# A two-layer block with four token mixers: 512-column products for values and output, fourteen merge-gate pairs ahead of the attention, one score scale on GpSimd

## The chip, the core and the metric

The kernel runs on one core of a Trainium2 chip. TensorE (PE) multiplies, VectorE (DVE), ScalarE (ACT) and GpSimd (POOL) do the elementwise work, SyncE's queue (SP) issues the DMAs. The metric is the device time of one execution in microseconds; a kernel's figure is the median of its runs.

## The reference

Two layers of the following, on 1024 tokens of width 1024, all in float32. `x` goes in, `x + rms_norm(merged @ w_o)` comes out.

```python
h = rms_norm(x, g_pre)
parts = jnp.split(h @ w_in, IN_SPLITS, axis=-1)          # a_u, a_v, ..., c_v, ..., m_z
y_a = chunked_gmlp(a_u, a_v, ...) * silu(a_z)            # local gated MLP on chunks of 128 tokens
y_b = nsa_attention(...) * silu(b_z)                     # compressed + selected + window of 256, three gates
y_c = forgetting_attention(...) * silu(c_z)              # causal, with forget gates
y_m = memory_attention(...) * silu(m_z)                  # 256 memory tokens
up = jnp.einsum('bsnw,nwd->bsnd', ys, w_br)              # four branches, 512 -> 1024 each
gates = sigmoid(jnp.einsum('bsd,dne->bsne', h, w_gate))  # four gates of 1024 x 1024
merged = jnp.einsum('bsnd,bsnd->bsd', gates, up)
return x + rms_norm(merged @ w_o, g_post)
```

## The kernel before, in words

Each float32 operand is split into two parts (`hi`, rounded to the type that TensorE takes, and `lo`, the rest), and a product is three matmuls: hi·hi, hi·lo, lo·hi (`mm3`, L240). A weight comes as a block of 128 x 1024 by DMA into `wr` (2 buffers), ACT makes `wh` (L220), POOL makes `wl` (L222); both have 3 buffers. For the names in `mk` and `mv` (the memory weights) POOL makes only the first half of `wl`, DVE the second (L224). An accumulation takes one PSUM bank of 512 columns: 2 banks `pj` and 3 banks `s`.

A layer runs through these stages, in program order; a scheduler at build time interleaves them and fixes each engine's order:

1. `front`: the memory's keys and values, the pre-norm of the tokens into `hh`, `hl` (two halves of 512 tokens).
2. `gates`: the values of the gated MLP (`gmlp_v`, names `av`) and of the forgetting attention (`put_values`, names `cv`), each in two column halves of 256; per half and for each of 8 token tiles 24 matmuls of 256 columns (`proj_t`, L271). `token_sums` meanwhile makes sums of the tokens on POOL, ACT and POOL, in four steps that stand between these projections. `gmlp_w` loads and splits the MLP's mixing weights (`wsr`, `wsh`, `wsl`, `ab`). Then `FRONT`, a list of gate pairs (n, e): `gate_pair` computes two gate blocks (n, e) and (n, e+1) for all tokens with 7 quarter products of 12 matmuls instead of 8, by sums of tokens and of weights (`weight_sums`), and stores them to DRAM (`thd`). After each pair a further small piece runs (`among`: the forget gates, then eight `gmlp_mix`).
3. `attention`: the compression, the forgetting attention (`fox`), projections, then the three-way attention (`nsa`, 64 units over both layers). In an NSA unit the selected and the window scores are exponentiated on ACT, scaled by 1/sum times a gate on DVE (`scale`, L640), turned by TensorE (L597), split by ACT and DVE, and multiplied with the values (L609). Between the units' matmuls stand those of `FILL`: names of independent projections. `u`, `c`, `m`, `b` finish branches; `w` and `y` are single gate blocks of branch 0 and 2 (`gate_early`), 48 matmuls of 512 columns each. A pace rule ties them evenly to the marks of the attention's score matmuls.
4. `merge`: four `add_branch`, which load the stored gates, or compute a gate that is not yet made, and sum; then `out_proj` for two token halves: four column quarters of `wo`, for each 4 token tiles of 24 matmuls with 256 columns.

Before, `FRONT` has 9 pairs (18 blocks) and `FILL` 13 single blocks; the 32nd, (2, 5), is computed in the merge.

`order_slots` (L167) adds a rule for all tiles of one pool: the first write of a tile waits for the first write of the tile that the program asked for before it in the same place.

## Time and profile before

| | us |
|---|---|
| median of 3 runs (lowest, highest) | 3187.17 (3183.8, 3191.8) |
| the profiled execution | 3185.2 |
| its span in the trace | 3183.4 |
| busy: PE, DVE, ACT, POOL | 3071.0, 1845.6, 1484.6, 1433.3 |

The profiled execution took 1.8 us more than its span and lies 2 us under the median. Matmuls are pipelined: one with 512 columns is shown as some 390 ns long although the next starts much sooner, so PE's busy time is a union of overlapping rows, and what a matmul costs is read from the distance of two starts. L numbers are lines of the kernel before.

### The profile page before, as it was taken

What the parts mean: (1) busy time and instruction counts of PE and PEld (TensorE: products, weight loads), DVE (VectorE), ACT (ScalarE), POOL (GpSimd) and SP (SyncE); (2) the same over time, 40 slices, a digit from 0 to 9 for tenths busy, and PEclk for the clock granted to TensorE, in tenths of its full rate; (3) what the DMA queues carried; (4) which work ended last, traced back from release to release, by engine and by line L of the source; (5) the groups of instructions that cost most, each with busy time, mean ns of one, the idle gap of its engine ahead of it and who ended that gap; (6) DMA issues with size and microseconds to landing.
All of it is one profiled execution on the core that took longest, in us unless ns stands there. A gap on an engine that the chain in (4) does not pass through costs nothing.

```text
span 3183.4 us, 48317 instructions
## 1 busy us (share of the span) xinstructions
PE 3071.0 (96%) x16704; PEld 2633.9 (83%) x16704; DVE 1845.6 (58%) x4329; ACT 1484.6 (47%) x3393; POOL 1433.3 (45%) x1142
## 2 busy tenths in 40 slices
PE   6999999999999999999989999999999999999998
PEld 6978877887888888788989788888888888887888
DVE  6255447768666855336551554477685678554363
ACT  4333335556556555313443433455665556552132
POOL 6744445543232323258557444445432333232673
PEclk9999999999999999999999999999999999999999
DMA  6334485654334322456553344955632342225454
GB/s 206 101 116 133 135 249 172 189 179 131 103 104 147 109 90 93 149 173 197 193 180 105 113 135 146 276 160 175 192 123 83 107 153 99 98 90 184 156 185 140
DMA packets 251685, 466.96 MB, mean 147 GB/s; under 512 B 42512, under 2 KB 100880, under 8 KB 251440
## 3 DMA queue, kind: packets, MB, share of 16 engines
q1 hardware_dynamic: 251440, 463.87, 45.7%
q8 instruction: 132, 2.16, 0.3%
q14 instruction: 113, 0.93, 0.1%
HBM read 326.35 MB, written 137.43 MB: 146 GB/s over the span
## 4 chain that ended last, share of the span: by engine, by line
PE 78%; DVE 5%; POOL 5%; issue 4%; DMA 4%; ACT 3%; SPq 1%; DVEq 0%; POOLq 0%; ACTq 0%
PE pj L244 12%; PE pj L248 12%; PE pj L247 12%; PE s L247 6%; PE s L244 6%; PE s L248 6%; PE s L447 5%; PE o L609 5%; PE pt L597 5%; PE pj L447 4%; PE s L565 3%; PE s L566 3%; POOL wl L222 2%; DVE p L638 1%; POOL acc L1291 1%
## 5 line engine op out<-in xcount | busy, mean ns | idle before, releaser
L222 POOL TENSOR_TENSOR wl<-wr,wh 128x1024 fp32r<-128x1024 f32 (+1 forms) x216 | 515.9, 2392 | 646.5 <-ACT wh L220 562.5
L244 PE MATMUL pj<-hh,wh 128*128 128x512 f32 x1648 | 651.4, 395 | 2.6 <-DVE z L317 1.5
L248 PE MATMUL pj<-hh,wl 128*128 128x512 f32 x1648 | 651.4, 395 | 1.6 <-POOL wl L222 1.6
L247 PE MATMUL pj<-hl,wh 128*128 128x512 f32 x1648 | 649.7, 394 | 0.0
L575 ACT ACTIVATE p<-p,nm 128x384 f32<-128x384 f32 (+3 forms) x512 | 306.8, 601 | 204.3 <-DVE nm L570 201.3
L308 DVE TENSOR_TENSOR pt<-pt,pt 128x512 fp32r<-128x512 f32 (+1 forms) x464 | 292.4, 635 | 147.7 <-ACT pt L306 146.1
L248 PEld LDWEIGHTS pj<-hh,wl 128*128 128x128 f32 x1648 | 310.2, 188 | 61.6 <-POOL wl L222 2.5
L244 PEld LDWEIGHTS pj<-hh,wh 128*128 128x128 f32 x1648 | 310.8, 189 | 60.8 <-DVE z L317 2.4
L247 PEld LDWEIGHTS pj<-hl,wh 128*128 128x128 f32 x1648 | 310.4, 188 | 57.7
L306 ACT ACTIVATE pt<-pt 128x512 fp32r<-128x512 f32 (+1 forms) x464 | 251.9, 554 | 222.8 <-PE pt L597 162.2
L220 ACT ACTIVATE wh<-wr 128x1024 fp32r<-128x1024 f32 x216 | 228.4, 1057 | 248.0 <-PE pj L247 84.8
L609 PE MATMUL o<-pt,v 128*128 128x512 f32 (+1 forms) x864 | 245.2, 370 | 7.6 <-DVE pt L308 7.3
L618 POOL TENSOR_TENSOR yt<-yt 128x256 f32<-128x256 f32 x128 | 100.6, 786 | 292.7 <-ACT yt L617 232.8
L597 PE MATMUL pt<-ident,p 128*128 128x128 f32 x1488 | 230.9, 272 | 0.3
L597 PEld LDWEIGHTS pt<-ident,p 128*128 128x128 f32 x1488 | 184.9, 140 | 42.5 <-DVE pt L308 0.7
L244 PE MATMUL s<-yh,wh 128*128 128x512 f32 x512 | 199.9, 393 | 7.1 <-ACT yh L306 5.3
L247 PE MATMUL s<-yl,wh 128*128 128x512 f32 x512 | 201.0, 393 | 1.5 <-DVE yl L310 1.4
L248 PE MATMUL s<-yh,wl 128*128 128x512 f32 x512 | 200.3, 391 | 0.0
L565 PE MATMUL s<-kd,q 128*128 128x512 f32 (+2 forms) x512 | 187.5, 369 | 13.1 <-DVE nm L570 13.1
L566 PE MATMUL s<-kl,q 128*128 128x512 f32 (+2 forms) x512 | 175.7, 345 | 0.0
L609 PEld LDWEIGHTS o<-pt,v 128*128 128x128 f32 x864 | 147.6, 188 | 32.0 <-DVE pt L308 12.3
L640 DVE TENSOR_SCALAR p<-p,r,sg 128x384 f32<-128x384 f32 (+2 forms) x320 | 167.0, 577 | 1.7
(370 smaller groups left out, 7143.1 us busy)
## 6 DMA issues: line engine op xcount, KB each, us to landing
wr<-wt SPq DMA_DIRECT2D x234, 512.0 KB
th<-thd SPq DMA_DIRECT2D x124, 256.0 KB
thd<-gu SPq DMA_DIRECT2D x72, 256.0 KB
q<-rq SPq DMA_DIRECT2D x32, 512.0 KB
yf<-y SPq DMA_DIRECT2D x64, 256.0 KB
thd<-th SPq DMA_DIRECT2D x52, 256.0 KB
vd<-vs SPq DMA_DIRECT2D x48, 256.0 KB
v<-vd SPq DMA_DIRECT2D x24, 512.0 KB
```

The source lines that it names most:

```text
L222: nc.gpsimd.tensor_sub(lo[:, :n], raw[:, :n], hi.bitcast(F32)[:, :n])
L244: ins = nc.tensor.matmul(out, ah, bh, start=k == 0, stop=False)
L247: nc.tensor.matmul(out, ah, bl, start=False, stop=False)
L248: nc.tensor.matmul(out, al, bh, start=False, stop=k == n - 1)
L306: self.last_act = nc.scalar.activation(hi, src, AF.Copy, scale=scale)
L308: (nc.gpsimd if pool else nc.vector).tensor_sub(lo, src, hi.bitcast(F32))
L447: nc.tensor.matmul(out, w[a][:, k], t[b][:, k], start=start and k == x == 0, stop=k == 3 and x == 2, skip_group_check=True)
L565: self.mark(nc.tensor.matmul(ps[:, :w], q[:, tq], kd[:, b0:b0 + w], start=True, stop=False), 1 + n / 128)
L566: nc.tensor.matmul(ps[:, :w], q[:, tq], kl[:, b0:b0 + w], start=False, stop=True)
L575: nc.scalar.activation(p[:, :n], p[:, :n], AF.Exp, bias=init, scale=-1.0, accum_out=l[:, x:x + 1])
L597: nc.tensor.transpose(pt[:, off + x * 128:off + x * 128 + 128], src, self.ident)
L609: nc.tensor.matmul(o[:, :, t0:t0 + m], it["v"], w[:, :, off:off + m], start=first, stop=last)
```

## The change

- `av`, `cv` and `wo` are laid out in full 512 columns, four blocks of two k-slices each (form "C"), and go through a new `proj_wide`: for four token tiles it holds four PSUM banks at once and goes through the weight's four parts; the bank of a tile is complete with the last part. It is called once per token half (so each `av` and `cv` weight is loaded twice) or, for `wo`, once per column half and token half.
- `wl` of `av` and `cv` is made half by POOL and half by DVE.
- `gmlp_w` stands behind the first `gmlp_v` instead of ahead of it.
- `FRONT` has 14 pairs (all of n = 0, 3, 1 and (2, 0), (2, 2)), `FILL` keeps the four single blocks y4 to y7.
- The window's scale in an NSA unit runs on GpSimd.
- The squares of the output go to a tile of their own instead of the bank's other half.

```diff
@@ gates
-    for h in range(2):
-        wide(f"cv{h}", "in", OFF["c_v"] + h * 256 + r(256))
-        wide(f"av{h}", "in", OFF["a_v"] + h * 256 + r(256))
+    full("cv", "in", OFF["c_v"] + r(512))
+    full("av", "in", OFF["a_v"] + r(512))
...
-FILL = "u0 y6 y7 c0 y0 u1 w2 w3 m0 c1 b0 u2 w4 y1 m1 w5 c2 b1 u3 w6 w7 m2 y2 b2 c3 y3 m3 y4"
+FILL = "u0 y6 c0 u1 m0 c1 b0 u2 y7 m1 c2 b1 u3 m2 y4 b2 c3 m3 y5"
-FRONT = [(0, 0)] + [(n, e) for n in (3, 1) for e in range(0, 8, 2)]
+FRONT = [(n, e) for n in (0, 3, 1) for e in range(0, 8, 2)] + [(2, 0), (2, 2)]
...
-        n = 512 if name[:2] in ("mk", "mv") else 1024
+        n = 512 if name[:2] in ("mk", "mv", "av", "cv") else 1024
...
+    def proj_wide(self, name, hi, lo, done, tail=False):
+        v = "p (k c) -> p k c"
+        ps = [self.pj() for _ in range(4)]
+        for parts in ((0,), (1,), (2, 3)) if tail else ((0,), (1,), (2,), (3,)):
+            w = [(x, [z.rearrange(v, c=512) for z in self.weight(f"{name}_{x}")]) for x in parts]
+            for i in range(4):
+                ts = slice(i * 128, i * 128 + 128)
+                for x, (wh, wl) in w:
+                    for k in range(2):
+                        kk = 2 * x + k
+                        for n, (a, b) in enumerate(((hi, wh), (hi, wl), (lo, wh))):
+                            self.nc.tensor.matmul(ps[i], a[:, kk, ts], b[:, k], start=kk == n == 0, stop=kk == 7 and n == 2)
+                if parts[-1] == 3:
+                    done(i, ps[i])
...
-                    nc.vector.tensor_scalar(t[:, :n], t[:, :n], r[:, x:x + 1], gate[x], op0=OP.mult, op1=OP.mult)
+                    by.tensor_scalar(t[:, :n], t[:, :n], r[:, x:x + 1], gate[x], op0=OP.mult, op1=OP.mult)
...
-        items[first]["pre"] = lambda: self.scale(win, l[:, 1], gate(1))
+        items[first]["pre"] = lambda: self.scale(win, l[:, 1], gate(1), pool=True)
...
-    def gmlp_v(self, half):
-        w = self.b_form(f"av{half}")
-        for i in range(8):
+    def gmlp_v(self, c):
+        def done(i, ps):
             t = self.st("gv")
-            self.gelu2(t[:, :256], self.proj_t(w, i), 256)
-            self.nc.sync.dma_start(self.gvd[i, :, half * 256:half * 256 + 256], t[:, :256])
+            self.gelu2(t, ps, 512)
+            self.nc.sync.dma_start(self.gvd[c * 4 + i], t)
+        self.proj_wide("av", self.hh[c], self.hl[c], done)
...
-        self.gmlp_w()
         self.gmlp_v(0)
         next(sums)
+        self.gmlp_w()
         self.gmlp_v(1)
...
-        for q in range(4):
-            wh, wl = self.b_form(f"wo{q}")
-            qs = slice(q * 256, q * 256 + 256)
-            for i in range(4):
-                ts = slice(i * 128, i * 128 + 128)
-                ps = self.pj()
-                self.mm3(ps[:, :256], [(hi[:, k, ts], lo[:, k, ts], wh(k), wl(k)) for k in range(8)])
+        for q in range(2):
+            qs = slice(q * 512, q * 512 + 512)
+            def done(i, ps):
+                sq = self.pcs.tile([128, 512], F32, name="sq", tag=("co", "si")[i % 2])
                 with self.hot():
-                    nc.vector.tensor_mul(ot[i // 2][:, i % 2, qs], ps[:, :256], gp[:, qs])
-                    nc.scalar.activation(ps[:, 256:], ps[:, :256], AF.Square, accum_out=ss[i][:, q:q + 1])
+                    nc.vector.tensor_mul(ot[i // 2][:, i % 2, qs], ps, gp[:, qs])
+                    nc.scalar.activation(sq, ps, AF.Square, accum_out=ss[i][:, q:q + 1])
+            self.proj_wide(f"wo{q}", hi, lo, done, tail=c == q == 1)
```

Three places of the engines' order, before and changed (lines are those of each kernel's own text).

ACT before, where the first values of the MLP are ready; `hh_501` are token splits of the pre-norm, `wsh` is the split of the mixing weights in `gmlp_w`, `ge` the first and third step of a gelu.

```order
L220 ACTIVATE wh<-wr 128x1024
L365 ACTIVATE x<-x,rstd 128x512 x2
L306 ACTIVATE hh_501<-pt 128x4x128 x5
L306 ACTIVATE wsh<-wsr 128x512
L324 ACTIVATE ge<-s 128x256
L326 ACTIVATE ge<-ge 128x256
L324 ACTIVATE ge<-pj 128x256
```

ACT in the changed kernel, from the last gelu of the first token half to the first of the second; `t1h` to `t4h` are splits of the token sums.

```order
L350 ACTIVATE ge<-ge 128x512
L330 ACTIVATE t2h<-w2r 128x512
L330 ACTIVATE t1h<-x_762 128x512
L330 ACTIVATE t3h<-w2r 128x512
L330 ACTIVATE t4h<-w2r 128x512
L227 ACTIVATE wh<-wr 128x1024 x4
L330 ACTIVATE wsh<-wsr 128x512
L348 ACTIVATE ge<-pj 128x512
```

The split `wsh`, which stood ahead of all gelus, now stands ahead of those of the second half, and behind four weight splits.

SP before, in the same place; `ab` is the bias of the mix, `gvd` the store of a gelu.

```order
L1000 DMA wsr<-ws 128x512
L217 DMA wr<-wt 128x1024
L301 DMA mvd<-mv 128x2x128 x2
L751 DMA co<-cos 64x512
...
L217 DMA wr<-wt 128x1024
L1002 DMA keep<-keep 128x128
L1012 DMA ab<-bs 128x512
L1032 DMA gvd<-gv 128x256 x7
```

SP in the changed kernel.

```order
L224 DMA wr<-wt 128x1024 x5
L1061 DMA gvd<-gv 128x512 x4
L224 DMA wr<-wt 128x1024 x2
L1030 DMA wsr<-ws 128x512
L1032 DMA keep<-keep 128x128
L224 DMA wr<-wt 128x1024
L1042 DMA ab<-bs 128x512
```

The loads of `gmlp_w` moved behind seven weight loads and the first half's four stores; `ab` is still the last DMA ahead of the stores of the gelus that follow it in the program.

POOL before, at the start of an NSA stretch of the first layer; `yt` are the head sums, `z` a branch's gate product.

```order
L618 TENSOR_TENSOR yt<-yt 128x256
L620 TENSOR_TENSOR yt<-yt 64x256
L222 TENSOR_TENSOR wl<-wr,wh 128x1024
L618 TENSOR_TENSOR yt<-yt 128x256
L620 TENSOR_TENSOR yt<-yt 64x256
```

POOL in the changed kernel, the same stretch.

```order
L642 TENSOR_TENSOR yt<-yt 128x256
L644 TENSOR_TENSOR yt<-yt 64x256
L665 TENSOR_SCALAR p<-p,r,sg 128x128
L665 TENSOR_SCALAR p<-p,r,sg 128x256
L229 TENSOR_TENSOR wl<-wr,wh 128x1024
L642 TENSOR_TENSOR yt<-yt 128x256
L644 TENSOR_TENSOR yt<-yt 64x256
L665 TENSOR_SCALAR p<-p,r,sg 128x384 x2
```

Two scales per unit are added to POOL's queue, between its weight splits and the head sums.

## Rows read from the trace of the kernel before

**Rows 1.** The page: busy us (share of the span) and instructions of each engine.

```profile
PE 3071.0 (96%) x16704; PEld 2633.9 (83%) x16704; DVE 1845.6 (58%) x4329; ACT 1484.6 (47%) x3393; POOL 1433.3 (45%) x1142
```

**Rows 2.** Busy time by stretch: values (both layers), gate pairs, fox, NSA, NSA's selection.

```profile
core 0: us, PE busy (x) PEld busy (x) DVE busy (x) ACT busy (x) POOL busy (x), PEclk, DMA share, GB/s
51.80:160.00 108.20, 92.81 (x747) 91.61 (x746) 33.68 (x65) 39.08 (x80) 79.61 (x57) 0.94 0.35 106
1636.60:1739.00 102.40, 94.26 (x752) 93.25 (x752) 23.58 (x52) 34.78 (x72) 76.17 (x53) 0.97 0.36 109
195.80:389.80 194.00, 186.98 (x862) 153.82 (x861) 111.08 (x171) 78.78 (x129) 92.36 (x72) 0.99 0.35 115
452.10:725.40 273.30, 268.00 (x1435) 225.50 (x1434) 201.58 (x558) 154.85 (x368) 127.53 (x148) 1.00 0.63 188
725.40:1282.70 557.30, 553.13 (x2912) 468.79 (x2910) 378.59 (x1064) 315.93 (x849) 173.83 (x138) 1.00 0.34 110
2600.00:2650.00 50.00, 50.00 (x268) 42.42 (x268) 48.14 (x140) 32.98 (x121) 17.81 (x16) 1.00 0.42 140
```

**Rows 3.** Timeline of PE in the output product: two matmuls twenty starts apart.

```profile
3116.89 0.28 PE L244 MATMUL pj<-wh,mhh 128*128 128x256 f32 x1
...
3119.29 0.28 PE L248 MATMUL s<-wh,mhl 128*128 128x256 f32 x1
```

**Rows 4.** Timeline of PE in the merge: two matmuls twenty-four starts apart.

```profile
2960.17 0.39 PE L248 MATMUL s<-yh,wl 128*128 128x512 f32 x1
...
2965.61 0.39 PE L248 MATMUL pj<-hh,wl 128*128 128x512 f32 x1
```

**Rows 5.** PE's waits at the values, layer one, layer two: us, times, longest.

```profile
PE s L244 <- DVE gv L327: 12.3, 2, 10.4
PE s L244 <- DVE gv L327: 6.6, 2, 4.3
```

**Rows 6.** Timeline at the first layer's first gelu, all engines.

```profile
75.49 0.63 ACT L306 ACTIVATE wsh<-wsr 128x512 fp32r<-128x512 f32 x1 [3.31 <-POOL wsr L1003]
76.15 1.08 DVE L308 TENSOR_TENSOR wsl<-wsr,wsh 128x512 fp32r<-128x512 f32 x1 [3.25 <-ACT wsh L306]
77.30 0.33 SPq L1012 DMA_DIRECT2D ab<-bs  x1
80.64 0.38 ACT L324 ACTIVATE ge<-s 128x256 f32<-128x256 f32 x1 [4.52 <-DMA ab<-bs]
82.43 0.58 PE L244 MATMUL s<-wh,hh 128*128 128x256 f32 x1 [10.42 <-DVE gv L327]
```

**Rows 7.** Busy time in the 5.6 us behind that wait, columns as in rows 2.

```profile
82.40:88.00 5.60, 5.57 (x27) 5.57 (x28) 2.53 (x6) 2.60 (x7) 0.00 (x0) 0.52 0.21 70
```

**Rows 8.** Groups by line and form, POOL: half a weight's split, a token sum.

```profile
L222 POOL TENSOR_TENSOR wl<-wr,wh 128x512 fp32r<-128x512 f32 x16 | 24.4, 1530 | 12.7 <-ACT wh L220 11.7 <-PE pt L371 0.7
L407 POOL TENSOR_TENSOR w2r<-hh,hl 128x512 f32<-128x512 f32 x32 | 40.7, 1293 | 7.2 <-DVE hl L308 7.2
```

**Rows 9.** Groups by line and form, DVE: the commonest gated scale.

```profile
L640 DVE TENSOR_SCALAR p<-p,r,sg 128x384 f32<-128x384 f32 x128 | 76.2, 626 | 0.7
```

**Rows 10.** Groups by line and form, POOL: products of two tensors, a fill.

```profile
L618 POOL TENSOR_TENSOR yt<-yt 128x256 f32<-128x256 f32 x128 | 100.6, 786 | 292.7 <-ACT yt L617 232.8 <-issue 58.3 <-POOL yt L620 1.5
L1172 POOL TENSOR_TENSOR z<-z,oo 128x512 f32<-128x512 f32 x48 | 63.1, 1315 | 153.1 <-DVE z L317 120.9 <-PE pt L597 13.5 <-PE s L248 10.6
L818 POOL MEMSET vcm<- 128x512 f32 x2 | 1.1, 526 | 0.0
```

**Rows 11.** Timeline: two scales beside a POOL instruction, and two without one.

```profile
1073.27 3.01 DVE L640 TENSOR_SCALAR p<-p,r,sg 128x384 f32<-128x384 f32 x2
1073.68 2.39 POOL L222 TENSOR_TENSOR wl<-wr,wh 128x1024 fp32r<-128x1024 f32 x1 [4.32 <-ACT wh L220]
2424.62 0.86 DVE L640 TENSOR_SCALAR p<-p,r,sg 128x384 f32<-128x384 f32 x2
```

**Rows 12.** Groups by line and form, PE: the turning of scores.

```profile
L597 PE MATMUL pt<-ident,p 128*128 128x128 f32 x1488 | 230.9, 272 | 0.3
```

More of the change, by code (lines that the diff above doesn't have):

```diff
@@ L53, in wide, with full @@
             plan[f"{name}_{half}"] = (src, f"B{half}", np.asarray(c))
+    def full(name, src, c):
+        for part in range(4):
+            plan[f"{name}_{part}"] = (src, f"C{part}", np.asarray(c))
     for h in range(4):
@@ L87, in weight_plan @@
             plan[f"u{n}{e}"] = ("br", "U", (n, e))
-    for q in range(4):
-        wide(f"wo{q}", "o", q * 256 + r(256))
+    for q in range(2):
+        full(f"wo{q}", "o", q * 512 + r(512))
     return plan
@@ L111, in lay_weights @@
                 o.reshape(128, 8, 128)[:, :, ok] = t
+            elif form[0] == "C":
+                k = 2 * int(form[1])
+                t = src[s][:, c].reshape(8, 128, 512)[k:k + 2]
+                o.reshape(128, 2, 512)[:] = t.transpose(1, 0, 2)
             else:
@@ L621, in head_out, with scale @@
         nc.sync.dma_start(dst[r, j * 256:(j + 1) * 256], t[r, 0])
-    def scale(self, pcs, l, gate=(None, None)):
+    def scale(self, pcs, l, gate=(None, None), pool=False):
         nc = self.nc
+        by = nc.gpsimd if pool else nc.vector
         r = self.psm.tile([128, 2], F32, name="r")
@@ L645, in put_values, with value_tile @@
         for i in range(8):
-            self.value_tile(w, i, h0)
-    def value_tile(self, w, i, h0):
-        ps = self.proj_t(w, i)
+            self.value_tile(self.proj_t(w, i), i, h0)
+    def value_tile(self, ps, i, h0):
         t = self.st("vs", R32).rearrange("p (h d) -> p h d", d=128)
@@ L653, in value_tile, with fox_values @@
         self.move(self.vd[h0:h0 + 4, :, i, :].rearrange("h p d -> p h d"), t)
+    def fox_values(self, c):
+        def done(i, ps):
+            for x in range(2):
+                self.value_tile(ps[:, x * 256:x * 256 + 256], c * 4 + i, x * 4)
+        self.proj_wide("cv", self.hh[c], self.hl[c], done)
     def get(self, pool, src, name):
@@ L1202, in gates @@
         next(sums)
-        self.gmlp_w()
         self.gmlp_v(0)
         next(sums)
+        self.gmlp_w()
         self.gmlp_v(1)
         next(sums)
-        self.put_values("cv0", 0)
+        self.fox_values(0)
         next(sums)
-        self.put_values("cv1", 4)
+        self.fox_values(1)
         next(sums, None)
@@ L1216, in gates @@
         for k, (n, e) in enumerate(FRONT):
-            self.gate_pair(n, e, w, lambda: self.gmlp_mix(k - 1) if k else self.forget())
+            self.gate_pair(n, e, w, lambda: self.gmlp_mix(k - 1) if 0 < k <= 8 else None if k else self.forget())
     def attention(self):
@@ L1233, in attention @@
                 self.gmlp_u(h)
-            elif name[0] in "wy":
-                self.gate_early({"w": 0, "y": 2}[name[0]], h)
+            elif name[0] == "y":
+                self.gate_early(2, h)
             else:
@@ L1307, in out_proj, with done @@
         ot = [self.pyh.tile([128, 2, 1024], F32, name="ot", tag="yh") for _ in range(2)]
-        ss = [self.psm.tile([128, 4], F32, name="oss") for _ in range(4)]
-        for q in range(4):
-            wh, wl = self.b_form(f"wo{q}")
-            qs = slice(q * 256, q * 256 + 256)
-            for i in range(4):
-                ts = slice(i * 128, i * 128 + 128)
-                ps = self.pj()
-                self.mm3(ps[:, :256], [(hi[:, k, ts], lo[:, k, ts], wh(k), wl(k)) for k in range(8)])
+        ss = [self.psm.tile([128, 2], F32, name="oss") for _ in range(4)]
+        for q in range(2):
+            qs = slice(q * 512, q * 512 + 512)
+            def done(i, ps):
+                sq = self.pcs.tile([128, 512], F32, name="sq", tag=("co", "si")[i % 2])
                 with self.hot():
-                    nc.vector.tensor_mul(ot[i // 2][:, i % 2, qs], ps[:, :256], gp[:, qs])
-                    nc.scalar.activation(ps[:, 256:], ps[:, :256], AF.Square, accum_out=ss[i][:, q:q + 1])
+                    nc.vector.tensor_mul(ot[i // 2][:, i % 2, qs], ps, gp[:, qs])
+                    nc.scalar.activation(sq, ps, AF.Square, accum_out=ss[i][:, q:q + 1])
+            self.proj_wide(f"wo{q}", hi, lo, done, tail=c == q == 1)
         for i in range(4):
```

## The prediction

> **What bounds the kernel now.** I read the page's busy line first [rows 1]. PE is busy for 3071.0 of the 3183.4 us, 96%; no other engine passes 58%. That is an average over unlike stages, so I read the same sums by stage next [rows 2]. The reader is to see that PE is the limit in every long stage: 186.98 of 194.00 us at the gate pairs, 268.00 of 273.30 at fox, 553.13 of 557.30 in an NSA stretch. The exception is the values: PE idles 15.4 of 108.20 us in layer one and 8.1 of 102.40 in layer two. So two kinds of edit can shorten the kernel: fewer or cheaper matmuls anywhere, and shorter idle time at the values. An edit that only moves elementwise work can do harm, or free an engine that PE waits for, and in NSA PE waits for next to nothing.
>
> What a matmul costs comes third, from the distance of starts. Twenty starts of 256 columns take 3119.29 − 3116.89 = 2.40 us, 0.120 us each [rows 3]. Twenty-four starts of 512 columns take 2965.61 − 2960.17 = 5.44 us, 0.227 us each [rows 4].
>
> **Wide products.** Two matmuls of 256 columns cost 0.240 us, one of 512 costs 0.227: 0.013 us saved per pair. A layer's values are 2 names x 2 column halves x 8 tiles x 24 = 768 matmuls of 256 columns, the output 4 x 8 x 24 = 768 too. Over both layers 3072 become 1536, and 1536 x 0.013 = 20.0 us of PE. The rows are of the output itself and of the stage ahead of it, so I take the whole. The Trainium skill speaks against this term (TensorE: Matmul & The Clock Gate, section "Back-to-back issue gap"): in its formula for the full clock a matmul takes its columns over 2.4 GHz plus a fixed 2.5 ns, so two narrow ones would exceed a wide one by 2.5 ns alone. By that the term would be an estimated 4 us. The rows have a difference of 13 ns per pair, and the measurement decides.
>
> The wide form loads each `av` and `cv` weight twice, 16 blocks a layer instead of 8. POOL makes only half of each `wl` now, and half a split takes 1.53 us [rows 8]; 16 x 1.53 = 24.5 us stand where 8 whole ones of 2.39 us at least [rows 11] took 19.1. POOL is the busiest elementwise engine there, 79.61 of 108.20 us [rows 2], and gets 5 us more. DVE, at 33.68, gets the other half. Both fit under PE.
>
> **Gates.** A pair is 7 x 12 = 84 matmuls of 512 columns, 19.07 us of PE at 0.227. Two single blocks are 96. Per layer five pairs are added ahead of the attention: 5 x 84 x 0.227 = 95.3 us. Ten single blocks go: nine from the attention, all in NSA (9 x 48 x 0.227 = 98.1 us), and (2, 5) from the merge (10.9). Net 109.0 − 95.3 = 13.7 us per layer, 27.2 over both (120 matmuls). A pair needs weight sums and evacuations: the stage of nine pairs has 111.08 us of DVE, 78.78 of ACT and 92.36 of POOL [rows 2], so 12.3, 8.8 and 10.3 per pair beneath 19.07 of PE. They are hidden; without that cover the largest would cost 12.3 x 5 per layer. The stores of ten more blocks fall where DMA is 35% busy, and the loads in the merge replace the computing of one block.
>
> **The wait at the values.** Before, PE waits 12.3 us in layer one and 6.6 in layer two for the first gelus [rows 5]. The timeline shows the chain [rows 6]: `wsh` at 75.49, `wsl` at 76.15, then by the slots' order the DMA of `ab` at 77.30, whose arrival releases the first gelu at 80.64; PE goes on at 82.43. ACT holds `wsh` ahead of all gelus, so no bank of the values comes free. PE then runs at half clock: the granted clock is 0.52, that is 1.2 of 2.4 GHz, and 27 matmuls start in 5.6 us [rows 7], where 5.6 / 0.120 = 47 would; 20 x 0.120 = 2.4 us lost. Counted in both layers: 12.3 + 6.6 + 4.8 = 23.7 us.
>
> After, four gelus and their stores go first, and `gmlp_w` stands ahead of the second half's gelus instead. Behind the waiting gelu on ACT stand the later gelus, and PE waits for their banks: `proj_wide` takes four of the five at once. From `wsh` to the gelu took 80.64 − 75.49 = 5.15 us, from the gelu to PE another 1.79. The fifth bank covers six matmuls, 1.36 us. If ACT comes to `wsh` just as the second half's first bank is complete, PE waits 5.15 + 1.79 − 1.36 = 5.6 us, and 2.4 follow at half clock: 8.0 per layer, 16.0 in all, 7 less than before. If `wsh` runs 5.15 us earlier, since its load and the four weights ahead of it arrive early, the whole 23.7 is gained; if POOL's 79.61 + 5 us of work become the limit, PE waits longer than before, up to the 12.3 + 2.4 of layer one in both layers (about 5 lost). I take −7: the order puts `wsh` directly ahead of that gelu.
>
> **NSA.** Without nine blocks PE's work falls from 557.3 to 459.2 us, while the vector work stays. DVE gives up 64 window scales a layer; the commonest takes 0.626 us [rows 9], so I take 38 at most off 378.59. 341 of 459.2 is 74%. The nearest stage with that share is fox, 201.58 of 273.30, also 74%, where PE idles 5.3 us, 1.9%. 1.9% of 459 is 8.7 where NSA had 4.2: 5 us more per layer, +10 in all. Below: +0, since in 50 us of NSA DVE worked 48.14 and PE all 50.00 [rows 2]. Above: +15 per layer, if PE's cover is missing where the scales crowd, three times the middle.
>
> **The scale on GpSimd.** No row shows a tensor_scalar on POOL. With 384 columns the nearest rows bound it [rows 10]: a fill of 512 in 0.526 gives 0.39 us, a product of two tensors 0.786 at 256 and 1.315 at 512, so 1.05. I take 0.75, between one input and two. 64 of them are 48 us per layer (25 to 67), and POOL's 173.83 us become some 220 of 459. It waits less, but not for long: the rest of its queue there, `wl` and head sums, comes later by one scale each. PE waited 0.3 us in all over 1488 turnings [rows 12], so the scaled scores are there early; one some 0.2 us later costs nothing. The cost is taken as 0 with that cover. A cost may fall on DVE: two scales beside a weight split on POOL took 3.01 us, without one 0.86 [rows 11]. The Trainium skill has a rule for this (SBUF — State Buffer, section "Who interferes with whom"): DVE and GpSimd share one pair of ports under an exclusive lock. The trace agrees in 3.01 against 0.86.
>
> **The sum.** −27.2 (gates) −20.0 (products) −7 (values) +10 (NSA) = −44.2. From the profiled 3185.2, which holds 1.8 us around its span, that is 3141; that execution lies 2 us under the median, so **3143**.
>
> **Rivals.**
> - *The wait vanishes and NSA stays full.* For it: POOL and DVE have room, and 48.14 of 50.00. Against: the order at `wsh`. −27.2 −20.0 −23.7 + 0 = −71: 3116.
> - *The values gain nothing*, because the wait only moves, or POOL binds: −27.2 −20.0 + 5 + 10 = −32: 3155.
> - *NSA gets loose*: DVE's peaks are no longer covered, +30 instead of +10, with no gain at the values: −27 −20 + 0 + 30 = −17: 3170.
> - *The wide product does not save what the rows show*: with 2.5 ns per pair the 20.0 become 4: 3159. Speaking against it: the two distances come from rows of like streams, 150 us apart.
> - *Slower*: POOL's scales lock DVE out for their whole length. 64 x 0.75 = 48 us come onto DVE per layer, 341 + 48 = 389. If DVE could not be filled past fox's 74%, NSA would take 389 / 0.74 = 526 instead of 459, +67 per layer, and the kernel would end near 3187 + 134 − 54 = 3267. It decides from 27 us per layer, where the other terms' 54 are used up. Against it stand the 48.14 of 50.00 us, and that POOL's present 173.83 us in NSA do not stop PE.
>
> **How the numbers follow.** Chances: the forecast 0.68 (its own range 3125 to 3162); wait gone 0.10; values gain nothing 0.11; NSA loose 0.05; 2.5 ns per pair 0.02; slower 0.04. The range is 3116 to 3168, the sum with the bounds of its terms: the case without the wait below, and above all but the last of the loose NSA. Within 0.3% (9.6 us, about what a measurement of this kernel can tell from no change) only mishaps of the loose case's kind at twice its size would end: 0.04. Faster has 0.92, slower 0.04.
>
> **What the changed profile would show.** The wide products right: starts of 512 columns 0.227 us apart at the values and the output, and no 256-column matmuls there. Gates right: 14 pairs at 19 to 20 us, PE over 95% busy in them. Values: a wait of PE for `gv` in the second half, some 6 us long and after it a clock near 0.52; no such wait would mean the better rival, a longer one or POOL near 100% the worse. NSA: 455 to 475 us long with PE's share at 98%; over 490, or `p` of the pool's scale as what PE's turning waits for, would speak for the slower rivals. The prediction is wrong if PE's total falls by much other than 47 us, or if its idle time, 112.4 us now, leaves 90 to 140.

## The result, and the profile after

The changed kernel took 3218.97 us (median of 4 runs, 3211.23 to 3222.48), the kernel before 3189.49 beside it: ratio 1.0088, 95% interval 1.0069 to 1.0108. One of the four runs behind that 3189.49 took 4343.96 us, far outside the other three (3183.8 to 3191.8, median 3187.17), and the ratio goes by the undisturbed runs alone. By the ratio the change costs some 28 us, by the median without that run 32; 3143 was forecast. The profiled execution took 3211.23 us; its span is 3209.1. L numbers are lines of each kernel's own text.

The page's busy line of the changed kernel, to be read against [rows 1]:

```profile
PE 3052.7 (95%) x15048; PEld 2539.6 (79%) x15048; DVE 1904.5 (59%) x4259; ACT 1508.9 (47%) x3369; POOL 1588.8 (50%) x1336
```

PE has 1656 matmuls fewer, as the change asks, but its busy time fell by 18.3 us only, not by 47, and its idle time rose from 112.4 to 156.4. The stages tell where. Busy time by stretch of the changed kernel, columns as in [rows 2]: values of layer one up to the first pair, the fourteen pairs, NSA of layer one and of layer two, from the last score of layer one to the first pair of layer two, and from the last score to the end.

```profile
50.00:190.20 140.20, 126.49 (x541) 101.61 (x540) 56.59 (x79) 53.84 (x89) 99.06 (x74) 0.95 0.50 154
190.20:480.00 289.80, 281.96 (x1280) 233.48 (x1279) 147.33 (x215) 110.08 (x185) 138.13 (x107) 0.98 0.35 113
815.20:1304.10 488.90, 465.08 (x2463) 389.18 (x2461) 355.31 (x1003) 295.03 (x819) 195.55 (x189) 0.99 0.33 104
2412.20:2901.80 489.60, 464.37 (x2465) 388.35 (x2463) 355.40 (x1003) 293.73 (x817) 194.18 (x187) 0.99 0.33 104
1304.10:1791.40 487.30, 453.44 (x2096) 373.99 (x2097) 233.60 (x333) 173.04 (x290) 299.08 (x203) 0.97 0.57 180
2901.80:3209.10 307.30, 293.63 (x1308) 240.96 (x1306) 140.41 (x192) 92.61 (x150) 170.40 (x104) 0.99 0.55 175
```

The kernel before in the same stretches at the values, the turn and the end (pairs and NSA stand in [rows 2]):

```profile
50.00:195.80 145.80, 129.56 (x940) 123.33 (x939) 41.32 (x80) 49.62 (x100) 94.16 (x67) 0.95 0.40 123
1282.70:1774.80 492.10, 467.73 (x2883) 419.74 (x2882) 214.30 (x345) 170.19 (x327) 287.77 (x190) 0.98 0.52 169
2859.70:3183.40 323.70, 306.57 (x1714) 266.95 (x1712) 138.87 (x206) 95.21 (x178) 167.12 (x100) 0.98 0.50 164
```

The reader is to see three things. The pairs cost what was forecast: 289.80 − 194.00 = 95.8 us per layer for five more (95.3 forecast). NSA gave back 68.4 and 67.8 us, not 93: it lasts 489, not 464, and PE idles 23.8 us in it instead of 4.2. And the three stretches with wide products became shorter by 5.6, 4.8 and 16.4 us, though at the turn and at the end the gate block (2, 5), 10.9 us of matmuls, left the merge as well.

PE's waits in the first NSA stretch: who waited for whom, us in all, times, longest.

```profile
PE o L633 <- DVE pt L332: 9.5, 6, 3.7
PE s L589 <- DVE nm L594: 6.0, 6, 1.7
PE o L629 <- DVE pt L332: 4.3, 5, 1.6
PE s L930 <- DVE pc L932: 1.9, 1, 1.9
```

These are the links of a unit's own chain: `nm` is the maximum of the scores, whose bank the next scores need, and `pt` the split of the turned scores, which the product with the values needs. Before, the same view had one wait of PE for `nm` and none for `pt`:

```profile
PE s L565 <- DVE nm L570: 2.9, 1, 2.9
```

The longest wait of the changed kernel in the timeline of all engines:

```profile
892.15 1.48 POOL L665 TENSOR_SCALAR p<-p,r,sg 128x384 f32<-128x384 f32 x2 [2.89 <-DVE r L653]
892.21 4.60 DVE L665 TENSOR_SCALAR p<-p,r,sg 128x512 f32<-128x512 f32 x4
...
893.59 2.47 POOL L229 TENSOR_TENSOR wl<-wr,wh 128x1024 fp32r<-128x1024 f32 x1
...
896.73 0.68 DVE L341 SCALAR_TENSOR_TENSOR z<-z,pj 128x512 f32<-128x512 f32 x1
897.32 0.68 DVE L1163 TENSOR_REDUCE mm<-s 128x2 f32<-128x512 f32 x1
...
897.92 1.27 DVE L332 TENSOR_TENSOR pt<-pt,pt 128x512 fp32r<-128x512 f32 x2
898.65 0.73 PE L633 MATMUL o<-pt,v 128*128 128x512 f32 x2 [3.70 <-DVE pt L332]
```

Four selection scales take 4.60 us on DVE beside POOL's work; the split that PE wants stands behind them in DVE's queue. PE, whose last matmul started at 894.68, has no filling matmul in its order there. In the 4.4 us behind this wait (898.60 to 903.00) the granted clock is 0.67.

### The profile page after: what moved, and what is told of

Same layout as the page of the kernel before. It is cut to its first block, busy times and chain, and to the rows that moved or that the text cites. A ratio compares the mean times of both kernels' runs of the same rounds, so it can differ in the third digit from the quotient of the medians.

```text
span 3209.1 us, 45404 instructions
## 1 busy us (share of the span) xinstructions
PE 3052.7 (95%) x15048; PEld 2539.6 (79%) x15048; DVE 1904.5 (59%) x4259; ACT 1508.9 (47%) x3369; POOL 1588.8 (50%) x1336
## 4 chain that ended last, share of the span: by engine, by line
PE 77%; DVE 9%; POOL 4%; issue 4%; DMA 3%; ACT 2%; SPq 1%; DVEq 0%; POOLq 0%; ACTq 0%
PE s L471 9%; PE pj L251 8%; PE pj L254 8%; PE pj L255 8%; PE pj L471 7%; PE s L300 5%; PE o L633 4%; PE s L254 4%; PE s L251 4%; PE s L255 4%; PE pt L621 4%; PE pj L300 3%; PE s L589 3%; PE s L590 2%; DVE p L665 1%
## 5 line engine op out<-in xcount | busy, mean ns | idle before, releaser
L229 POOL TENSOR_TENSOR wl<-wr,wh 128x1024 fp32r<-128x1024 f32 (+1 forms) x212 | 477.3, 2254 | 283.4 <-ACT wh L227 257.5
L251 PE MATMUL pj<-hh,wh 128*128 128x512 f32 x1328 | 526.9, 397 | 2.1 <-DVE z L341 2.1
L255 PE MATMUL pj<-hh,wl 128*128 128x512 f32 x1328 | 524.3, 395 | 0.0
L254 PE MATMUL pj<-hl,wh 128*128 128x512 f32 x1328 | 523.7, 394 | 0.0
L255 PEld LDWEIGHTS pj<-hh,wl 128*128 128x128 f32 x1328 | 250.5, 189 | 50.0
L251 PEld LDWEIGHTS pj<-hh,wh 128*128 128x128 f32 x1328 | 251.4, 189 | 48.2 <-DVE z L341 2.6
L254 PEld LDWEIGHTS pj<-hl,wh 128*128 128x128 f32 x1328 | 251.0, 189 | 46.0
L633 PE MATMUL o<-pt,v 128*128 128x512 f32 (+1 forms) x864 | 253.3, 379 | 26.3 <-DVE pt L332 26.0
L463 POOL TENSOR_TENSOR wl<-ws,wh 128x512 fp32r<-128x512 f32 x112 | 154.2, 1390 | 125.2 <-ACT wh L462 125.1
L665 POOL TENSOR_SCALAR p<-p,r,sg 128x384 f32<-128x384 f32 (+2 forms) x128 | 95.3, 753 | 191.1 <-DVE r L653 115.5
```

The lines of the kernel that those rows point to most:

```text
L229: nc.gpsimd.tensor_sub(lo[:, :n], raw[:, :n], hi.bitcast(F32)[:, :n])
L251: ins = nc.tensor.matmul(out, ah, bh, start=k == 0, stop=False)
L254: nc.tensor.matmul(out, ah, bl, start=False, stop=False)
L255: nc.tensor.matmul(out, al, bh, start=False, stop=k == n - 1)
L633: nc.tensor.matmul(o[:, :, t0:t0 + m], it["v"], w[:, :, off:off + m], start=first, stop=last)
```

## The experiments

Times are medians; the ratio is to the kernel before on the same chip, with its 95% interval.

| kernel | edit | us | ratio |
|---|---|---|---|
| e1 | changed, scale on DVE | 3230.06 | 1.0120 (1.0103 to 1.0137) |
| e2 | before, scale on GpSimd | 3192.60 | 1.0004 (0.9994 to 1.0014) |
| e3 | before, fourteen pairs | 3239.39 | 1.0156 (1.0139 to 1.0173) |
| e4 | before, wide products | 3181.99 | 0.9978 (0.9967 to 0.9989) |
| e5 | changed, eleven pairs | 3209.73 | 1.0063 (1.0047 to 1.0079) |
| e6 | before, idle work on DVE | 3196.75 | 1.0010 (0.9996 to 1.0023) |
| e7 | e3, the window's scale left out | 3213.37 | 1.0078 (1.0058 to 1.0099) |
| e8 | before, wide output alone | 3192.03 | 1.0008 (0.9996 to 1.0020) |
| e9 | e3, three steps of the selection's ranking left out | 3233.40 | 1.0144 (1.0110 to 1.0178) |
| e10 | changed, more filling at group starts | 3195.25 | 1.0017 (1.0003 to 1.0031) |
| e11 | e4, wide output in layer two alone | 3177.97 | 0.9966 (0.9955 to 0.9977) |
| e12 | e11, low parts of the values' weights on DVE | 3165.65 | 0.9926 (0.9903 to 0.9948) |
| e13 | e12, mixing weights behind both halves | 3168.50 | 0.9943 (0.9928 to 0.9958) |
| e14 | e13 with pairs, GpSimd scale and e10's pace | 3190.50 | 1.0006 (0.9996 to 1.0016) |
| e15 | e12, mask's product on DVE | 3162.36 | 0.9914 (0.9890 to 0.9937) |

### The parts one by one: e1 to e4

e1 is the changed kernel with this line; e2 is the kernel before with its opposite:

```diff
-        items[first]["pre"] = lambda: self.scale(win, l[:, 1], gate(1), pool=True)
+        items[first]["pre"] = lambda: self.scale(win, l[:, 1], gate(1))
```

e3 is the kernel before with the changed `FRONT`, `FILL` and the condition on `among`; e4 is e1 with `FRONT` and `FILL` of before, that is all the rest of the change.

> The changed kernel with the window's scale back on DVE; the wide products, the fourteen pairs and the thin filling of NSA stay. The changed kernel's first NSA stretch (first compressed score to last score) takes 488.9 us with PE idle 23.8 of it, where the kernel before took 557.3 with 4.2; the sum had asked for 464. Theory A, GpSimd's scales slow DVE's (a scale of 512 columns on DVE went from 623 to 834 ns, and all DVE work in the stretch fell by 23 us instead of 38) and come late themselves: the stretch falls to some 465 to 470 us, the kernel to about 3175. Theory B, the matmuls that covered NSA's elementwise chains are gone and DVE binds: DVE gets 15 to 23 us per layer more, so the stretch stays at 489 or grows to 500, the kernel lies at 3219 to 3240.

> The kernel before with one edit: the window's scale on GpSimd. All nine blocks still fill NSA. Theory A in its strong form (GpSimd's scale is a loss wherever it stands): the stretch of 557.3 us grows by 10 to 25 us per layer, the kernel to some 3210 to 3240. Theory B (the cover decides, the engine of the scale does not): PE stays busy for 553 of 557 us, the kernel within 0.3% of 3187. If GpSimd's scale costs only where the cover is thin, this one stays at 3187 and the one with the scale back on DVE gains.

> The kernel before with one edit: fourteen pairs ahead of the attention and four single blocks in its filling; values and output in 256 columns, scale on DVE. The count of matmuls asks for 27 us less over both layers. Theory A: the NSA stretch comes out at 459 to 470 us, the kernel at 3160 to 3175. Theory B: the stretch stays near 490 with DVE at 77% and PE idle some 25 to 30 us in it, so two times 25 us eat the gain, the kernel at 3200 to 3225.

> The kernel before with the wide products alone: values and output in 512 columns, their weights' second halves on DVE, the mixing weights' load behind the first half of the values; nine pairs, thirteen single blocks and the scale on DVE as before. The prediction asked for 20.0 us of matmul time and 7 us of the values' wait, 3160. In the changed kernel's trace the values' stretch became only 5.6 us shorter in layer one, the way from the last score of layer one to the first pair of layer two no shorter than the gate block taken out of it, the end some 11 us: by that reading 17 us less, 3170. If the waits for the low halves of the weights (20 us of PE's waits) and the late memory norm at the layer's turn eat all of it: 3187.

The first NSA stretch of e1, e2 and e3, in this order, columns as in [rows 2]:

```profile
813.40:1309.80 496.40, 470.14 (x2469) 392.00 (x2468) 374.21 (x1066) 296.15 (x816) 149.62 (x127) 0.98 0.33 103
```

```profile
723.50:1279.80 556.30, 550.18 (x2893) 466.44 (x2892) 352.49 (x1000) 316.58 (x848) 215.85 (x200) 1.00 0.34 110
```

```profile
823.40:1322.30 498.90, 469.94 (x2483) 392.07 (x2481) 376.93 (x1068) 299.24 (x824) 151.81 (x129) 0.99 0.33 103
```

Theory A (GpSimd's scale is the loss) falls: without it the changed kernel is 11 us slower, not faster (the intervals of the two ratios just touch, and NSA is 7.5 us longer in layer one), and put alone into the kernel before it changes nothing. Theory B stands, and the loss is larger than it said (3200 to 3225): the pairs alone cost 48 us, and their NSA lasts 499, with PE idle 29 us. Cover, here and below, means matmuls that PE can do while a chain of dependent elementwise steps runs; the filling is full with thirteen single blocks and thin with four. The parts add up. Against 3191.12 the pairs give +48.3 and the wide products −9.1; the scale on GpSimd gives 3218.97 − 3230.06 = −11.1 on the thin filling. Together that is +28, and +28 to +32 was measured. Each part missed: −17 was forecast for the pairs (−27 and +10 in NSA), −27 for the wide products, which came out between the two readings of e4.

### Load of DVE or length of the chain: e6, e7

e6 adds to the kernel before, e7 takes from e3:

```diff
+                    if twice:
+                        nc.vector.tensor_reduce(self.spare, t[:, :n], axis=AX.X, op=OP.max)
```

```diff
-        items[first]["pre"] = lambda: self.scale(win, l[:, 1], gate(1))
```

> The kernel before with idle work added on DVE alone: after each scale of a window a maximum over the scaled tile, which nobody reads, 64 per layer and some 35 to 40 us of DVE, so that DVE is as loaded in NSA (415 of 557 us, 75%) as with the fourteen pairs alone (377 of 499, 76%), but with all nine blocks of cover in place. If DVE's throughput is the bound (it can't be filled beyond 75% while PE goes on), PE idles as there, some 29 us per NSA instead of 4, and the kernel goes to 3230 or more. If it is the length of a unit's chain (scores, maximum, exponentials, scale, turning, split) against the matmuls that stand beside it, the time stays within 0.3 to 0.5% of 3191.

> Fourteen pairs alone, with the window's scale left out (the window's scores stay unscaled and ungated): 38 us of DVE per layer fall away and nothing takes their place. If DVE's throughput binds, NSA falls with it, from 499 to 460 to 470 us, and the kernel from 3239 to 3175. If it is the chain's length, the scale's 0.6 us of a chain of several us matter little: NSA at 485 to 492, the kernel at 3215 to 3225, as the scale on GpSimd gave (NSA 489).

The first NSA stretch of e6, and that of e7:

```profile
724.10:1282.90 558.80, 554.54 (x2910) 468.49 (x2909) 409.70 (x1127) 316.40 (x849) 174.58 (x138) 1.00 0.34 110
```

```profile
817.60:1300.20 482.60, 461.23 (x2470) 386.98 (x2469) 341.65 (x974) 295.06 (x814) 150.48 (x127) 1.00 0.33 106
```

In e6 DVE carries 409.70 us, 73% of the stretch, and PE idles 4.3 us, as before. In e3 DVE carries 376.93, 76%, and PE idles 29. The two shares are not quite the same, but with fewer blocks PE idles at lower shares too: 21.4 us in e7 with DVE at 71%, 19.7 us in e5 (next section) with DVE at 66%. So it is not how much DVE has to do that makes PE wait, but whether matmuls stand beside it. e7 takes away load and chain length at once: with 35 us less on DVE, NSA came down by 16 us, between the two theories but nearer to the chain; 21.4 us of idle PE remain. Shortening a chain helps where the cover is thin, by less than half of what is taken away.

### The dose: e5

```diff
-FRONT = [(n, e) for n in (0, 3, 1) for e in range(0, 8, 2)] + [(2, 0), (2, 2)]
+FRONT = [(0, 0), (0, 2), (0, 4)] + [(n, e) for n in (3, 1) for e in range(0, 8, 2)]
-FILL = "u0 y6 c0 u1 m0 c1 b0 u2 y7 m1 c2 b1 u3 m2 y4 b2 c3 m3 y5"
+FILL = "u0 y6 y7 c0 y0 u1 m0 c1 b0 u2 y1 m1 c2 b1 u3 w6 w7 m2 y2 b2 c3 y3 m3 y4"
```

> The changed kernel with eleven pairs ahead of the attention and nine single blocks in its filling (one in the merge), wide products and GpSimd scale kept: the dose between nine (wide products alone, 3182) and fourteen (3219). A single block taken out of NSA and made in a pair ahead saves 10.9 us and costs 9.5, so 1.36 us are won per block only if all 10.9 come off NSA. If every block of cover covers alike, each of the nine blocks costs the 24.6 us that the forecast of 464 lies below the 489 measured, divided by nine, 2.7 us, per layer, so four blocks less per layer lose 2 x 4 x (2.7 - 1.4) = 11 us against nine pairs: 3193. If the cover is only spent at the end (PE busy 553 of 557 before means that there is some to spare), the first four blocks are free: 3182 - 11 = 3171, and the exposed time of NSA is as with thirteen blocks, PE idle below 8 us per layer.

Neither number came. e5 lies 27.7 us above nine pairs (e4), where fourteen lie 37 above. Its first NSA stretch:

```profile
763.60:1296.60 533.00, 513.32 (x2701) 433.77 (x2699) 354.03 (x1001) 305.05 (x831) 204.05 (x193) 0.99 0.34 106
```

Four blocks are 43.6 us of matmuls; the stretch fell from 557.3 by 24.3, and PE idles 19.7. Two pairs more ahead of the attention cost 38.1 us, so each layer loses 13.8, which accounts for the 27.7. So there was no cover to spare: the first blocks taken away are exposed too. What is at stake is small: a block in a pair saves 10.9 − 9.5 = 1.4 us, so an eighth of a block exposed eats the gain, and here it was over four tenths (19.3 of 43.6).

### Where in NSA: e9, e10

e9 is e3 without three operations per ranking row; e10 is the changed kernel with a heavier mark:

```diff
-            nc.vector.tensor_tensor(gt, oth, own, op=OP.is_gt)
-            nc.vector.tensor_mul(ge, ge, v16(ch[:, 128:384]))
-            nc.vector.tensor_max(ge, ge, gt)
```

```diff
-                    self.mark(nc.tensor.matmul(ps[:, x, :], q[:, tq], self.kcm[:, g, :], start=True, stop=True), 1)
+                    self.mark(nc.tensor.matmul(ps[:, x, :], q[:, tq], self.kcm[:, g, :], start=True, stop=True), 3)
```

> Fourteen pairs alone, with three of the five operations of each ranking row of the selection left out (so other blocks are selected): 7.5 us of DVE per group of heads, 15 per layer, all at the start of a group, where DVE is 92 to 98% busy in the traces. Theory C, the shortage sits at the group starts (compressed scores, selection, first units), where DVE is full with and without the nine blocks and time can't shrink: NSA falls from 499 by some 10 to 15 us per layer, the kernel from 3239 to 3210 to 3220. Theory D, every unit lacks its share of cover: PE idles elsewhere as before, NSA falls by 3 to 6, the kernel to 3228 to 3233.

> The changed kernel with a mark of the compressed scores counted three times in the pace, so that more of the filling (not more in all) may stand at the group starts. Theory C: the three stretches there last 134 us per layer in all, with 112 us of matmuls where 127 stood before; they last that long anyway, so filling moved there comes off the rest, up to 15 us per layer: kernel from 3219 to 3190 to 3205. Theory D: what the group starts get the other units lack: 3215 to 3225.

The starts of the two groups of heads in layer one, cut at the same score matmuls (first group; last part of the first group and the compressed scores of the second; selection and first units of the second), of the kernel before, the changed one and e10:

```profile
725.40:777.20 51.80, 48.31 (x251) 40.16 (x250) 46.65 (x129) 34.51 (x119) 19.50 (x17) 0.97 0.44 143
977.40:1032.20 54.80, 54.80 (x297) 46.68 (x296) 37.22 (x99) 34.92 (x109) 19.09 (x16) 1.00 0.50 164
1032.20:1063.80 31.60, 31.60 (x168) 26.62 (x167) 31.12 (x86) 17.59 (x57) 11.51 (x9) 1.00 0.35 113
```

```profile
815.20:865.80 50.60, 46.58 (x236) 39.03 (x235) 45.55 (x126) 34.10 (x120) 21.11 (x20) 0.93 0.45 140
1041.90:1093.50 51.60, 49.41 (x276) 41.53 (x275) 38.74 (x96) 34.83 (x107) 20.50 (x19) 1.00 0.50 159
1093.50:1125.70 32.20, 28.32 (x140) 23.21 (x140) 29.62 (x83) 17.45 (x57) 17.11 (x15) 0.95 0.40 129
```

```profile
811.50:864.00 52.50, 52.50 (x278) 44.41 (x276) 45.00 (x126) 32.66 (x115) 21.32 (x19) 1.00 0.45 147
1036.20:1089.20 53.00, 51.98 (x286) 44.16 (x285) 34.70 (x94) 32.65 (x102) 19.58 (x18) 1.00 0.53 167
1089.20:1123.00 33.80, 33.06 (x172) 27.44 (x170) 32.86 (x84) 19.06 (x62) 18.58 (x17) 1.00 0.39 122
```

The three stretches last 138.2, 134.4 and 139.3 us, with 716, 652 and 736 matmuls. That is a quarter of NSA which hardly shrank when 64 matmuls were taken from it, and which holds 84 more (some 19 us at 0.227) for 5 us: time that the chains there take anyway. e10's 24 us against the changed kernel came as theory C said, though in the two profiled executions, whose spans differ by 17.1, only 5.3 and 9.6 us stand in the NSA stretches (now 483.6 and 480.0 long). The 19 us that went there for 5 should have given 14 in layer one; but the rest of the stretch, which they left, became 10 us shorter, not 19, so they were partly missed there as well. The other 2.2 of the 17.1 us stand outside NSA. e9 went as theory D said: with 14.7 us less on DVE its NSA takes 492.9 us in layer one, 6.0 less than e3, and the kernel 6 us less, with intervals that overlap. So DVE's own load is at most a part of what sets the group starts, though it is 92 to 98% busy in one. Together, as far as these runs show: the loss is one of cover by place. Both group starts and single units wait on their chains when matmuls are missing beside them, and moving the same filling about gains part of it back. Which link of the chain counts most was not separated.

### The wide products: e8, e11

e8 is the kernel before with `full("wo..")`, `proj_wide` and the changed `out_proj` alone. e11 keeps the wide values and uses the wide output only in the last layer:

```diff
+        last = self.l == self.depth - 1
+        if last:
+            for q in range(2):
...
+                self.proj_wide(f"wx{q}", hi, lo, done, tail=c == q == 1)
+        else:
+            for q in range(4):
+                wh, wl = self.b_form(f"wo{q}")
```

> The kernel before with the output product alone in 512 columns. The matmuls ask for 10 us less over both layers. In the kernel with both wide products the layer's turn grew by 4 us although its matmuls shrank by 10, and the end fell by 9. If the turn's loss comes from the output's four tiles that are done all at once (square, sum, power, store, then the next layer's norm of the memory and the tokens in line on DVE), this kernel shows it too: 3191 - 10 + 10 = 3186 to 3191. If it comes from the values (low halves late on POOL and DVE), this one gains the 10: 3181.

> The kernel before with wide values, and the wide output in the last layer alone (the first layer's output in 256 columns, so that the turn to layer two is as it was). Wide values and output together gave 3182 against 3191, the wide output alone 3192 with the turn 10 us longer and the end 8 us shorter. If the 8 us wait of PE at the turn belongs to the wide output, this kernel keeps the values' gain (some 10) and the end's 8: 3173. If the turn is late for another reason (the values' weights loaded ahead): 3182.

The output alone won nothing. Its turn and its end, to be read against 492.10 and 323.70 above:

```profile
1287.10:1789.80 502.70, 464.48 (x2500) 400.38 (x2499) 213.74 (x329) 167.13 (x295) 289.33 (x190) 0.97 0.52 165
2877.90:3193.20 315.30, 301.23 (x1329) 246.04 (x1327) 139.03 (x190) 91.65 (x146) 167.83 (x100) 0.98 0.52 169
```

The end is 8.4 us shorter, the turn 10.6 longer. PE in the changed kernel at the turn, the last product and the next instruction:

```profile
1608.78 0.39 PE L300 MATMUL pj<-wh,mhl 128*128 128x512 f32 x1
1617.14 0.66 PE L395 MATMUL pt<-ident,x 128*128 128x128 f32 x2 [7.97 <-issue]
```

PE stands 8 us at a turning of the next layer's normed memory. Its row gives no releaser; on DVE the steps of four output tiles, which the wide form completes within a few us of each other, and two low halves of weights stand ahead of the norm's steps. e8 has the same 7.97 us there; in e11 no wait of that length stands at the turn. So the wide output of layer one brings the wait; that it does so through DVE's order is read from the trace, not tested. e11 keeps the gain of the values and took 3177.97, between the 3173 of this reading and the 3182 of the other; its interval still overlaps that of e4, so the time alone does not settle it.

### The values: e12, e13, e15

```diff
-        n = 512 if name[:2] in ("mk", "mv", "av", "cv") else 1024
-        nc.gpsimd.tensor_sub(lo[:, :n], raw[:, :n], hi.bitcast(F32)[:, :n])
+        n = 512 if name[:2] in ("mk", "mv") else 0 if name[:2] in ("av", "cv") else 1024
+        if n:
+            nc.gpsimd.tensor_sub(lo[:, :n], raw[:, :n], hi.bitcast(F32)[:, :n])
```

```diff
-        self.gmlp_w()
         self.gmlp_v(1)
         next(sums)
+        self.gmlp_w()
```

```diff
-        nc.gpsimd.tensor_mul(f3(wr), f3(wr), keep[:, None, :].to_broadcast([128, 4, 128]))
+        nc.vector.tensor_mul(f3(wr), f3(wr), keep[:, None, :].to_broadcast([128, 4, 128]))
```

> The same with the low parts of the values' weights made on DVE alone instead of half by POOL. PE waits 9.3 us in layer one and some 7 in layer two for POOL's halves at the values. If POOL is late there because the token sums stand ahead of them in its queue, these waits go and nothing takes their place: some 10 to 16 us below the kernel beside it, 3160. If they only turn into waits for DVE, which then needs twice as long per weight and has the gelus and value splits behind it: no gain, 3173 or up to 10 us more.

> The kernel with the low halves on DVE (3166) with the mixing weights' load behind both halves of the values of the MLP, ahead of the forgetting attention's values, so that no gelu stands behind it. PE waits 9.8 us in layer one and 7.6 in layer two for the gelus of the second half there, and runs at half clock behind each wait. If these waits are the chain from the mixing weights through their bias's DMA to the gelu, they go: 17 us of waits and up to 5 us of clock, 3145 to 3150. If the gelus are late because ACT or DVE have no room (DVE now makes the low halves too), a wait of the same length stays, 3160 to 3166.

> The kernel with the low halves on DVE (3166), and in the load of the mixing weights the product with the mask on DVE instead of GpSimd. Moving the whole load behind both halves only moved the 8 to 10 us wait to the value splits. In the trace the mask's product ends at 107.3 us, behind two token sums of 4.5 us in GpSimd's queue, though its load had landed at some 103; ACT then stands idle 5.4 us before the split. If GpSimd's queue is the cause, about 4 us of each wait go: 3166 - 8 - some clock = 3155 to 3158. If the load itself (behind the weights in the DMA queue) is, nothing moves: 3166.

PE's waits at the values of layer one, of the changed kernel and of e12:

```profile
PE s L300 <- POOL wl L229: 6.0, 4, 2.9
PE pj L300 <- POOL wl L229: 4.5, 2, 3.3
PE pj L300 <- DVE gv L351: 3.0, 1, 3.0
```

```profile
PE pj L303 <- DVE gv L354: 9.8, 1, 9.8
PE s L303 <- DVE wl L234: 2.7, 3, 1.7
```

In the changed kernel the wait for the gelu is only 3 us, but POOL's low halves are late six times, 10.5 us: in its queue they stand among the token sums and their splits, of 1.25 to 1.75 us each. With these halves on DVE the kernel takes 12 us less than e11, within the 10 to 16 that were expected: PE comes through earlier, and then meets the gelu's wait at full length. Its chain in e12:

```profile
107.38 0.63 ACT L333 ACTIVATE wsh<-wsr 128x512 fp32r<-128x512 f32 x1 [5.42 <-POOL wsr L1036]
108.04 1.08 DVE L335 TENSOR_TENSOR wsl<-wsr,wsh 128x512 fp32r<-128x512 f32 x1 [4.29 <-ACT wsh L333]
109.18 0.33 SPq L1045 DMA_DIRECT2D ab<-bs  x1
112.26 0.60 ACT L351 ACTIVATE ge<-pj 128x512 f32<-128x512 f32 x1 [4.26 <-DMA ab<-bs]
```

This is the chain of [rows 6] again. e13 shows that it moves with the mixing weights: put behind both halves, they hold ACT ahead of the value splits, PE waits for those (7.6 us in layer one, 8.8 in layer two), and the time stays. e15 shows that GpSimd's queue is part of it: the wait in layer one fell from 9.8 to 8.4 us, that in layer two from 7.6 to 1.7; 3162.36 is the best of all, though not apart from e12 by the intervals. What is left is the load's place in the DMA queue and the DMA of `ab`, not tried further.

### The pairs on the mended kernel: e14

It is e13 with the changed `FRONT` and `FILL`, the scale on GpSimd and e10's mark.

> The same with the fourteen pairs, the scale on GpSimd and the pace that lets more filling stand at the group starts: the changed kernel with all mends. With the old places of the rest, the fourteen pairs with this pace and scale stood at 3195 where nine pairs stood at 3182, 13 us more. If the loss of cover in NSA is independent of the mends at the values and the turn, this kernel is 13 us (8 to 18) above the one beside it. If the pairs' loss was partly the mended waits, it is level or faster.

It lies 22 us above e13, more than the 13 (8 to 18) expected; by the intervals of the four ratios the two differences are not apart. Its NSA lasts 482.1 us in layer one with PE idle 17.7, much as in e10 (483.6 and 17.4). The pairs' loss is no smaller for the mends.

## Why the prediction was wrong

**Gates and NSA: the step that failed.** The matmuls were counted rightly: five pairs cost 95.8 us where 95.3 were forecast. What failed is "1.9% of 459 is 8.7 where NSA had 4.2: 5 us more per layer". I took the idle share of PE from fox, a stage with the same share of DVE, 74%. Measured were 23.8 us of 488.9, 15 more than the 8.7; and PE was busy for 465 us where 553.1 − 98.1 = 455 was left, 10 more, with a mean granted clock of 0.99 against 1.00. By the forecast's own terms NSA lost 25 us more per layer, 50 of the 76 us of the miss. The wide products missed by another 18 (e4); the 8 us that are left are about what the profiled execution, from which the 25 is read, lies under the median of its kernel (3211 and 3219). e6 shows why the share was the wrong thing to read: 73% on DVE costs nothing where matmuls cover it; 76% costs 25 us more of idle PE where nine blocks are gone (e3), and 66% costs 15 where four are gone (e5). The upper bound, +15 per layer, was too low as well, since it was a multiple of the same middle. The row with 48.14 us of DVE in 50.00 [rows 2] was read as proof that DVE can be full beneath PE. It shows that, but not what follows when PE's matmuls are taken away: the three stretches at the group starts above kept their 134 us with 64 matmuls fewer, so there the matmuls had filled time that the chain took anyway.

**The rivals.** "NSA gets loose" named the mechanism, at +30 for both layers and 0.05; +60 was measured (2 x 25 beyond the forecast's +10). The rival *Slower*, GpSimd locking DVE out, is not what made the kernel slower: the scale on GpSimd gains 11 us with the thin filling (e1) and nothing with the full one (e2). A contention is there, and it made the relief small. DVE fell by 23 us in NSA, not 38, and by 19 against e1, which has the same filling. Its own scales of 512 columns, in the mean of the changed kernel, of e1 and of the kernel before:

```profile
L665 DVE TENSOR_SCALAR p<-p,r,sg 128x512 f32<-128x512 f32 x96 | 79.9, 846 | 1.0
L665 DVE TENSOR_SCALAR p<-p,r,sg 128x512 f32<-128x512 f32 x96 | 65.0, 691 | 0.1
L640 DVE TENSOR_SCALAR p<-p,r,sg 128x512 f32<-128x512 f32 x96 | 57.9, 617 | 0.5
```

Of the 229 ns between the first and the last, 155 came with GpSimd's scales; the other 74 were there without them. With the full filling GpSimd's scales cost 86 (703 ns in e2).

On POOL the commonest scale took 0.80 us, where 0.75 was taken:

```profile
L665 POOL TENSOR_SCALAR p<-p,r,sg 128x384 f32<-128x384 f32 x96 | 76.0, 801 | 165.1 <-DVE r L653 99.3 <-DVE r L659 36.3 <-PE pt L621 15.0
```

The Trainium skill's rule on the shared ports (SBUF — State Buffer, section "Who interferes with whom") is in line with 846 against 691 ns; that the ports are the cause was not tested.

**Wide products.** The price per matmul held; nineteen rows of the output product, the first and the last:

```profile
3179.73 0.39 PE L300 MATMUL pj<-wh,mhh 128*128 128x512 f32 x1
...
3183.81 0.39 PE L300 MATMUL pj<-wl,mhh 128*128 128x512 f32 x1
```

Eighteen starts take 4.08 us, 0.227 each, so 1536 pairs save the 20 us. But the products alone (e4) gained 9, not 20 + 7. The sum had costed the tail of the output at nothing: completing four tiles together made PE wait 8 us at the turn, and e8, whose turn is 10.6 us longer, shows that this eats the output's gain. The rival on the price did not happen: what was lost was lost in waits. In the Trainium skill's formula for an isolated matmul (TensorE: Matmul & The Clock Gate, section "Back-to-back issue gap") two narrow matmuls cost only 2.5 ns more than a wide one; the distance of starts here, 240 against 227 ns, does not bear that out.

**Values.** The wait for the second half's gelu came as described but short, 3.0 us in layer one where 5.6 were forecast, because PE was already held up by POOL: "Both fit under PE" was wrong for POOL. The 5.6 was too small as well: with POOL's halves out of the way (e12) the wait is 9.8 us, since it begins 2 us before `wsh` does. Its load was counted, not its order: the low halves stand behind token sums in its queue. The rival "the values gain nothing, or POOL binds" is what happened there: that stretch won 5.6 us, of which 5 are matmuls.

## What to carry to other kernels

Filling matmuls that stand beside dependent elementwise chains are not free to take away: before moving work out of such a stage, compare what the move saves (here an eighth of a block) with the share of the stage that would be exposed, and find out by taking a few blocks away which part of the stage shrinks at all. The busy share of an engine does not tell this: DVE at 73% cost nothing with cover, and DVE at 66% came with 20 us of idle PE without it. And an edit that completes several tiles at once, or that adds work to a queue with long instructions in it, is costed by what stands ahead in each queue, not by the queue's total.

## What the runs showed of the hardware

Four DVE scales of 512 columns took 4.60 us beside GpSimd's scales and a weight split, against 4 x 0.617 = 2.5 by the mean of the kernel before. Leaving the window's scales out took 35 us off DVE in an NSA stretch (e3 to e7); moving them to GpSimd took 19 off with the same thin filling (e1 to the changed kernel) and 26 with the full one (the kernel before to e2).

A scale on GpSimd is not in proportion to its columns: 0.67 us for 128, 0.56 for 256, 0.80 for 384 in the means of the changed kernel, and 0.58, 0.58 and 0.77 in those of e2.

The two waits of PE looked at here cost more than their length: the granted clock was 0.67 in the 4.4 us behind the wait of 3.7, and 0.59 in the 4 us from 1617.00 on, behind the wait at the turn. The mean granted clock over the span was 0.984 in the changed kernel and 0.991 before.
